# Output projection of a two-layer decoder trunk: the last quarter's weights split once into big tiles, and one more norm step on VectorE

## The chip, the cores and the metric

The kernel runs on one core of one Trainium2 chip. The metric is the device time of one execution in microseconds (us). Before the change the median of three runs is 2775.11 us (2769.86 to 2777.68).

## The reference

The program is a decoder trunk of two layers on a sequence of 1024 tokens with 1024 channels, float32. Each layer has a token mixer and a channel mixer. What matters here is the end of the first and the start of the second:

```python
mix = jnp.einsum('bsd,de->bse', merged, w_o)            # output projection, 1024 x 1024 x 1024
x = layer_norm(ALPHA * x + mix, ln1_g, ln1_b)           # over the 1024 channels of each token
up = causal_dwconv(jnp.einsum('bsd,df->bsf', x, w_up), ffn_conv_w)   # 1024 x 5632
```

`layer_norm` subtracts the mean, divides by the root of the variance plus 1e-5, multiplies by a gain and adds a bias. There are two layers, so everything told below happens twice.

## The kernel before, in words

**Products in three passes.** A float32 operand is split into a rounded high half and a low half (`split`, lines 87 to 94): ScalarE (ACT) copies the source into a tile of the rounded type (line 90), then VectorE (DVE) or GpSimd (POOL) subtracts that copy from the source (line 94). A product is then three matmuls: high by high, high by low, low by high (`product`, lines 106 to 112).

**Tiles.** Every kind of tile has a fixed number of buffers: 14 of kind X (two 128 x 1024 halves each), 6 of kind w (one 128 x 1024 half, or both halves of a 128 x 512 block), 3 of kind ws (a loaded weight, 128 x 1024). PSUM has 8 banks of 128 x 512. A new tile takes a buffer whose last reader is done; its first writer waits for that.

**Output projection** (`output`, lines 628 to 671). There are eight token tiles t of 128 tokens, in two halves h of four. For each h the merged operand is split into four X tiles (`mt`). For each half of the output columns, eh, four accumulators collect over four weight blocks kp; a weight block is loaded by SyncE's queue (SP) into a ws tile, ACT makes the high half and POOL the low half, into two w tiles (`weight`, lines 96 to 104, called at line 645). So three of the four quarters (h, eh) load four blocks each. In the last quarter, h = 1 and eh = 1, the four token tiles are taken in two pairs, (4, 5) and then (6, 7), and each pair loads and splits the four blocks again: eight loads, eight high halves, eight low halves.

After a quarter with eh = 1 the token tiles are normalised (`norm`, lines 262 to 292). DVE adds alpha times the residual (line 663), takes the statistics (259, 267), subtracts the mean and multiplies by the gain (290); ACT takes the root (269); DVE refines the reciprocal in four short steps (271, 274 to 277); ACT multiplies by it (291); and the bias is added (292), for t = 7 by DVE and for the other seven by POOL. Norms are marked urgent, so the planner ranks them far ahead of their place in the text.

**The hand-over to the up projection.** The up projection is Strassen-like: its moving operands are 512 x 512 blocks and sums of blocks of the normalised tokens, transposed by TensorE and split. Tokens 0 to 3 give two blocks (`to_first`, B11 and B21, four X tiles in all). Tokens 4 to 7 give five (`to_second`, lines 311 to 326: T1, T2, B22, T3, T4, ten X tiles): per token three subtractions on DVE (321, 323, 324) and one on POOL (322) into two w tiles, then five groups of four transposes (298), each into a PSUM bank of its own, from which ACT takes a high and DVE a low half. Only when all four tokens have gone through it can the second part of the first pair run, since its matmuls move all 512 tokens.

The order on TensorE (PE) and on SP is that of the text. After the last quarter it is: first part of weight pair 0 (`begin`, line 716: 24 matmuls, on B11 and B21, one low half by POOL and one by DVE, and one bank added up at line 730); `to_second` for token 4; first part of pair 1; `to_second` for tokens 5, 6 and 7; second part of pair 0 (`rest`, line 732: four sums of weight blocks on POOL at lines 741 and 738, five more blocks split by `made`). The first weight of each pair and the second one are loaded at line 707 into ws tiles. The orders of DVE, ACT and POOL are made by a planner from ranks in the text and its own estimate of times, and are then fixed.

Of the kernel before, what the change touches and what calls it, by code (L numbers as in the profile page):

```python
# [11 lines left out]
F32 = mybir.dt.float32  # L12
F32R = mybir.dt.float32r
# [5 lines left out]
P = 128  # L19
# [41 lines left out]
class Trunk:  # L61
# [566 lines left out]
    def output(self, l, merged):  # L628

        nc = self.nc  # L630
        self.xc = {}
        zs, st = [None] * 8, {}
        for h in range(2):
            mt = []
            for kp in range(NKP):
                t = self.new([P, 2, 2, HALF], F32R, "X")
                self.split(t[:, 0], t[:, 1], merged[kp][:, :, h * HALF:(h + 1) * HALF])
                mt.append(t)
            for eh in range(2):

                groups = [(0, 1), (2, 3)] if h and eh else [(0, 1, 2, 3)]
                for group in groups:
                    acc = {}
                    for kp in range(NKP):
                        wh, wl = self.weight(self.ins["w_o"][l, eh, kp])
                        if kp == NKP - 1 and eh == 0:
                            for t in range(4 * h, 4 * h + 4):
                                zs[t] = self.new([P, D], F32, ("pt", "pt", "pt", "q", "s", "s", "s", "t")[t])
                                nc.sync.dma_start(zs[t][:], self.ins["x"][t] if l == 0 else self.spill[t])
                            if h == 0:  # L650
                                g, b = self.gains(l, 0)
                        for t in group:
                            if t not in acc:
                                acc[t] = self.bank()
                            ts = slice(t * P, (t + 1) * P)
                            self.product(acc[t][:], [
                                (mt[kp][:, 0, k, ts], mt[kp][:, 1, k, ts], wh[:, k * HALF:(k + 1) * HALF],
                                 wl[:, k * HALF:(k + 1) * HALF]) for k in range(2)], kp == 0, kp == NKP - 1)
                        if (kp or eh) and group[0] == 0:
                            self.pending()  # L660
                    for t in group:
                        z = zs[4 * h + t][:, eh * HALF:(eh + 1) * HALF]
                        nc.vector.scalar_tensor_tensor(z, z, ALPHA, acc[t][:], op0=ALU.mult, op1=ALU.add)
                        st[4 * h + t] = self.stats(zs[4 * h + t], (eh,), st.get(4 * h + t))
                    if eh:
                        for i in group:
                            t = 4 * h + i
                            with self.urgent():
                                self.norm(zs[t], g, b, "vector" if t == 7 else "gpsimd", st[t])
                            self.pend.append((lambda t=t, i=i: self.to_second(zs[i], zs[t], i, self.spill1[t])) if h else  # L670
                                             (lambda t=t, i=i: self.to_first(zs[t], i, self.spill1[t])))

# [428 lines left out]
```

## Time and profile before

| | before |
|---|---|
| median of 3 runs | 2775.11 us |
| profiled execution, its own time | 2775.4 us |
| its span | 2773.4 us |
| PE busy, share of the span | 93% |
| DVE, ACT, POOL busy | 69%, 44%, 53% |
| granted clock of PE, mean | 0.971 of full |

Times in the trace count from the start of the span. "Idle before" is the time that an engine stood still ahead of an instruction, and the arrow names what ended it. A line number is that of the program; 90 and 94 belong to the splitting helper, so the tile names tell what is split. The output projection of the first layer ends near 677 us and that of the second near 2055 us.

### The profile page before, as it was taken

The numbers are of one execution on the slowest core, as the hardware profiler recorded it, in microseconds if no ns is written. First come the engines' busy times: TensorE is split into PE (matmuls) and PEld (weight loads), VectorE is DVE, ScalarE is ACT, GpSimd is POOL, SyncE is SP. The second block draws the span as 40 slices with busy tenths as digits, with TensorE's granted clock in tenths as the row PEclk, the third lists the DMA queues.
The fourth block names the chain that finished last, engine by engine and source line by source line (L and its number), as shares of the span: only waits on it lengthen the run. The fifth ranks groups of instructions, "written<-read, shape, count | busy, mean of one in ns | idle before, by whom it ended". The sixth has DMA issues, their size and how long they took to land.

```text
span 2773.4 us, 32010 instructions
## 1 busy us (share of the span) xinstructions
PE 2583.8 (93%) x11408; PEld 2105.9 (76%) x11408; DVE 1919.5 (69%) x2310; ACT 1233.4 (44%) x2050; POOL 1457.2 (53%) x962
## 2 busy tenths in 40 slices
PE   5989999998899999899889999999988999998887
PEld 4868887787688888677667788777867888877676
DVE  6565556737887877786675656477478887767866
ACT  4434445523544554434444444454335455544343
POOL 2554456767466555370434545566674556553701
PEclk8999999999999999999899999999999999999999
DMA  3433358554133333674323423765532333327742
GB/s 123 138 114 107 108 196 225 161 181 150 57 104 114 114 99 107 222 277 134 106 95 117 142 75 108 237 189 164 201 122 75 96 107 103 114 92 266 267 139 76
DMA packets 163232, 389.59 MB, mean 140 GB/s; under 512 B 17408, under 2 KB 48896, under 8 KB 162048
## 3 DMA queue, kind: packets, MB, share of 16 engines
q1 hardware_dynamic: 136496, 293.02, 32.3%
q0 software_dynamic: 14848, 55.09, 7.0%
q10 hardware_dynamic: 11728, 39.45, 3.7%
q8 instruction: 89, 1.46, 0.2%
q14 instruction: 71, 0.58, 0.1%
HBM read 281.75 MB, written 104.43 MB: 139 GB/s over the span
## 4 chain that ended last, share of the span: by engine, by line
PE 49%; DVE 16%; issue 5%; DMA 3%; ACT 3%; POOL 3%; ACTq 0%; DVEq 0%; SPq 0%; POOLq 0%
PE b L111 16%; PE b L112 16%; PE b L110 16%; DVE w L94 3%; DVE X L94 2%; DVE st L259 1%; DVE ve L275 1%; DMA X<-in_w_down 1%; POOL ws L738 1%; DVE pt L811 1%; ACT w L90 1%; POOL w L94 1%; DVE t L290 1%; DMA X<-h_blocks 1%; DVE w L321 0%
## 5 line engine op out<-in xcount | busy, mean ns | idle before, releaser
L110 PE MATMUL b<-X,w 128*128 128x512 f32 x2552 | 1014.1, 397 | 55.1 <-ACT s L727 20.0
L112 PE MATMUL b<-X,w 128*128 128x512 f32 x2552 | 1008.3, 395 | 27.9 <-DVE w L94 18.6
L111 PE MATMUL b<-X,w 128*128 128x512 f32 x2552 | 1006.5, 394 | 3.2 <-DVE X L94 3.2
L94 DVE TENSOR_TENSOR w<-ws,w 128x512 fp32r<-128x512 f32 (+1 forms) x454 | 450.4, 996 | 358.5 <-ACT w L90 346.3
L90 ACT CAST w<-ws 128x512 fp32r<-128x512 f32 (+1 forms) x608 | 408.0, 677 | 489.6 <-PE b L112 154.5
L110 PEld LDWEIGHTS b<-X,w 128*128 128x128 f32 x2552 | 487.4, 191 | 167.5 <-ACT s L727 24.6
L112 PEld LDWEIGHTS b<-X,w 128*128 128x128 f32 x2552 | 486.9, 191 | 136.4 <-DVE w L94 22.5
L94 POOL TENSOR_TENSOR w<-ws,w 128x512 fp32r<-128x512 f32 (+2 forms) x154 | 297.5, 1934 | 532.5 <-ACT w L90 520.3
L111 PEld LDWEIGHTS b<-X,w 128*128 128x128 f32 x2552 | 487.3, 191 | 105.9 <-DVE X L94 5.5
L741 POOL TENSOR_TENSOR ql<-ws 128x512 f32<-128x512 f32 x82 | 125.0, 1524 | 354.8 <-DMA ws<-in_w_in 254.0
L111 PE MATMUL b<-w,w 128*128 128x512 f32 x528 | 214.4, 406 | 48.5 <-DVE w L94 41.3
L110 PE MATMUL b<-w 128*128 128x512 f32 x528 | 211.1, 400 | 2.7 <-DVE pt L905 1.4
L112 PE MATMUL b<-w,w 128*128 128x512 f32 x528 | 210.6, 399 | 0.0
L111 PEld LDWEIGHTS b<-w,w 128*128 128x128 f32 x528 | 102.0, 193 | 82.4 <-DVE w L94 54.3
L738 POOL TENSOR_TENSOR ws<-ws,ws 128x512 f32<-128x512 f32 x82 | 142.4, 1736 | 6.2
L811 DVE SCALAR_TENSOR_TENSOR q<-t,par,q 128x1023 f32<-128x1023 f32 x88 | 127.4, 1448 | 19.0 <-ACT q L808 18.1
L94 DVE TENSOR_TENSOR w<-X,w 128x512 fp32r<-128x512 f32 (+1 forms) x107 | 121.5, 1158 | 22.3 <-ACT w L90 22.3
L738 POOL TENSOR_TENSOR ws<-ql,ws 128x512 f32<-128x512 f32 x82 | 125.0, 1524 | 6.3
L738 POOL TENSOR_TENSOR ws<-ws 128x512 f32<-128x512 f32 x82 | 118.6, 1446 | 16.9 <-DVE w L94 12.7
L110 PEld LDWEIGHTS b<-w 128*128 128x128 f32 x528 | 102.0, 193 | 28.3 <-DVE t L905 2.7
L811 DVE SCALAR_TENSOR_TENSOR pt<-t,par,pt 128x1023 f32<-128x1023 f32 x88 | 123.3, 1401 | 0.2
L112 PEld LDWEIGHTS b<-w,w 128*128 128x128 f32 x528 | 102.1, 193 | 20.6
(242 smaller groups left out, 3783.6 us busy)
## 6 DMA issues: line engine op xcount, KB each, us to landing
ws<-in_w_up SPq DMA_DIRECT2D x88, 512.0 KB
ws<-in_w_in SPq DMA_DIRECT2D x75, 512.0 KB
gates<-t ACTq DMA_DIRECT2D x48, 512.0 KB
ws<-in_w_o SPq DMA_DIRECT2D x40, 512.0 KB
h_blocks<-t SPq DMA_DIRECT2D x80, 256.0 KB
s<-h_blocks SPq DMA_DIRECT2D x66, 256.0 KB
t<-gates SPq DMA_DIRECT2D x32, 512.0 KB
t<-q_parts POOLq DMA_DIRECT2D x64, 256.0 KB, 4.1
```

What stands on the lines that cost most here:

```text
L90: self.nc.scalar.copy(hi, src)
L94: return eng.tensor_tensor(lo, src, hi.bitcast(F32), op=ALU.subtract)
L110: self.nc.tensor.matmul(out, wh, xh, start=start and i == 0, stop=False, skip_group_check=more)
L111: self.nc.tensor.matmul(out, wh, xl, start=False, stop=False, skip_group_check=more)
L112: self.nc.tensor.matmul(out, wl, xh, start=False, stop=stop and i == n - 1, skip_group_check=more)
L259: self.nc.vector.bn_stats(st[:, c, :], z[:, c * HALF:(c + 1) * HALF])
L275: nc.vector.scalar_tensor_tensor(ve[:], ve[:], r[:], r[:], op0=ALU.mult, op1=ALU.mult)
L290: nc.vector.scalar_tensor_tensor(z[:], z[:], mv[:, 0:1], g[:], op0=ALU.subtract, op1=ALU.mult)
L738: sub = lambda out, x, y: nc.gpsimd.tensor_tensor(out, x, y, op=ALU.subtract)
L741: nc.gpsimd.tensor_tensor(s1[:], a21, a22, op=ALU.add)
L811: nc.vector.scalar_tensor_tensor(y[:, d:], c[:, :S - d], w(k), y[:, d:], op0=ALU.mult, op1=ALU.add)
```

## The change

In the last quarter the four weight blocks are loaded by the first pair of token tiles into ws tiles as before, but their halves are made into one X tile per block, which is held, and the second pair uses the held halves. Nothing else of that quarter's order on PE changes. The number of loads in it falls from eight to four. And the bias of token tiles 4, 5 and 6 is added by DVE too, as it was for token tile 7.

```diff
-                groups = [(0, 1), (2, 3)] if h and eh else [(0, 1, 2, 3)]
+                groups, held = [(0, 1), (2, 3)] if h and eh else [(0, 1, 2, 3)], {}
                 for group in groups:
                     acc = {}
                     for kp in range(NKP):
-                        wh, wl = self.weight(self.ins["w_o"][l, eh, kp])
+                        if len(groups) == 1:
+                            wh, wl = self.weight(self.ins["w_o"][l, eh, kp])
+                        elif kp not in held:
+                            held[kp] = self.new([P, 2, 1024], F32R, "X")
+                            wt = self.new([P, 1024], F32, "ws")
+                            nc.sync.dma_start(wt[:], self.ins["w_o"][l, eh, kp])
+                            wh, wl = held[kp][:, 0], held[kp][:, 1]
+                            self.split(wh, wl, wt[:], "scalar", "gpsimd")
+                        else:
+                            wh, wl = held[kp][:, 0], held[kp][:, 1]
...
-                                self.norm(zs[t], g, b, "vector" if t == 7 else "gpsimd", st[t])
+                                self.norm(zs[t], g, b, "vector" if h else "gpsimd", st[t])
```

## Rows read from the trace of the kernel before

**Rows 1.** Windows, layer 0; columns PE, PEld, DVE, ACT, POOL, granted clock, DMA share.
```profile
622.00:644.00 22.00, 22.00 (x102) 18.26 (x102) 18.68 (x36) 9.39 (x13) 13.89 (x6) 1.00 0.51 199
...
682.00:704.00 22.00, 17.86 (x66) 14.07 (x67) 22.00 (x32) 5.99 (x11) 17.11 (x10) 0.73 0.09 38
704.00:724.00 20.00, 14.36 (x75) 10.59 (x75) 16.81 (x27) 11.03 (x22) 1.29 (x1) 0.84 0.20 71
724.00:755.00 31.00, 30.44 (x132) 24.61 (x130) 24.07 (x23) 16.42 (x25) 15.59 (x10) 0.99 0.13 40
```

**Rows 2.** Timeline of PE, layer 0: start, length, engine, line, tiles, idle before and releaser.
```profile
647.79 0.50 PE L111 MATMUL b<-w,X 128*128 128x512 f32 x1 [2.47 <-POOL w L94]
...
676.47 0.39 PE L112 MATMUL b<-w,X 128*128 128x512 f32 x1
...
682.36 0.79 PE L112 MATMUL b<-X,w 128*128 128x512 f32 x1 [4.61 <-POOL w L94]
682.96 0.63 PE L110 MATMUL b<-X,w 128*128 128x512 f32 x1
683.38 0.63 PE L111 MATMUL b<-X,w 128*128 128x512 f32 x1
...
691.11 1.04 PE L298 MATMUL b<-ident,w 128*128 128x128 f32 x8
...
698.93 0.80 PE L110 MATMUL b<-X,w 128*128 128x512 f32 x1 [3.72 <-DVE X L94]
...
719.10 0.80 PE L112 MATMUL b<-X,w 128*128 128x512 f32 x1 [3.09 <-DVE w L94]
```

**Rows 3.** The same of PE in layer 1.
```profile
2060.45 0.79 PE L112 MATMUL b<-X,w 128*128 128x512 f32 x1 [4.61 <-POOL w L94]
...
2097.18 0.79 PE L112 MATMUL b<-X,w 128*128 128x512 f32 x1 [3.73 <-DVE w L94]
```

**Rows 4.** Timeline of POOL, layer 0.
```profile
638.97 2.39 POOL L292 TENSOR_TENSOR pt<-pt,t 128x1024 f32<-128x1024 f32 x1 [1.28 <-ACT pt L291]
...
675.50 5.14 POOL L292 TENSOR_TENSOR s<-s,t 128x1024 f32<-128x1024 f32 x2 [2.80 <-ACT s L291]
680.60 1.71 POOL L94 TENSOR_TENSOR w<-ws,w 128x512 fp32r<-128x512 f32 x1
```

**Rows 5.** Timeline of ACT, layer 0.
```profile
642.86 1.03 ACT L90 CAST w<-ws 128x1024 fp32r<-128x1024 f32 x1
...
674.27 2.19 ACT L291 ACTIVATE s<-s,r 128x1024 f32<-128x1024 f32 x2 [4.66 <-DVE r L277]
676.36 1.12 ACT L90 CAST w<-ws 128x512 fp32r<-128x512 f32 x2
```

**Rows 6.** Timeline of SP's queue, layer 0: issues of the loads.
```profile
624.95 39.32 SPq L102 DMA_DIRECT2D ws<-in_w_o  x8
666.66 88.97 SPq L707 DMA_DIRECT2D ws<-in_w_up  x8
```

**Rows 7.** Timeline of DVE, layer 0.
```profile
639.08 2.30 DVE L275 SCALAR_TENSOR_TENSOR ve<-ve,r 128x1 f32<-128x1 f32 x1
...
672.77 0.14 DVE L276 TENSOR_SCALAR ve<-ve 128x1 f32<-128x1 f32 x1
672.83 1.27 DVE L290 SCALAR_TENSOR_TENSOR s<-s,mv,t 128x1024 f32<-128x1024 f32 x1
...
678.36 2.82 DVE L321 TENSOR_TENSOR w<-s,pt 128x512 f32<-128x512 f32 x1
...
694.92 3.30 DVE L290 SCALAR_TENSOR_TENSOR t<-t,mv,t 128x1024 f32<-128x1024 f32 x1
...
702.41 1.21 DVE L292 TENSOR_TENSOR t<-t,t 128x1024 f32<-128x1024 f32 x1
...
706.27 0.68 DVE L321 TENSOR_TENSOR w<-t,q 128x512 f32<-128x512 f32 x1
...
707.59 6.06 DVE L94 TENSOR_TENSOR X<-b,X 128x512 fp32r<-128x512 f32 x10
```

## The prediction, made before the changed kernel ran

> **What bounds the kernel now.** PE is busy for 93% of the span, so the first question is where it is not. I read the windows of layer 0 around the end of the output projection first. From 622 to 644 us and again from 724 on PE is full (22.00 of 22, 30.44 of 31) at a granted clock of 1.00 and 0.99; from 682 to 724 it is busy 32.2 of 42, at 0.73 and 0.84 [rows 1]. That hand-over to the up projection is the only place that the change can speed up much. In it DVE is busy 22.00 of 22 and then 16.81 of 20, POOL 17.11 and then 1.29 [rows 1].
>
> PE's timeline says what it waits for [rows 2]. The last matmul of the output projection starts at 676.47, so PE is through at about 676.7. It waits 4.61 until 682.36 for POOL's low half of pair 0's first weight; 3.72 until 698.93 for DVE (a low half out of PSUM, by which a bank comes free); 3.09 until 719.10 for DVE (the low half of a weight of the second part of pair 0). Behind each wait matmuls start 0.42 apart instead of 0.23 (682.96 and 683.38, against 132 instructions in 30.44 us [rows 1, 2]): the lower of the two clock levels, 1.2 GHz; at 682.36 some 13 matmuls do, 13 x 0.2 = 2.6 us. Layer 1 is the same: its first wait ends at 2060.45, its last at 2097.18 [rows 3], 36.7 apart as in layer 0. So the stretch to shorten is 676.7 to 719.1, 42.4 us, twice.
>
> Why is POOL late at 677? Its low half of pair 0 starts at 680.60, behind the bias additions of tokens 4 and 5 (two in 5.14 us from 675.50) [rows 4]. These waited for ACT's multiplication at 674.27, and ACT for DVE's reciprocal; ACT's high halves for pair 0 stand behind it, at 676.36 [rows 5]. The load itself was issued at 666.66, after the eight of the last quarter, which had been spread over 39.32 us from 624.95 on [rows 6]. Inside the last quarter PE waits for no weight after 647.79 [rows 2]: the four repeated splits are not on its path. What they cost is what stands behind them and beside them.
>
> Beside them means DVE. The subtraction of line 321 took 2.82 us at 678.36 while POOL added biases, and 0.68 at 706.27 with POOL idle; line 290 took 3.30 at 694.92 and 1.27 at 672.83 [rows 4, 7].
>
> **The change, part by part.** The numbers are us per layer.
>
> *Four repeated loads, four high halves, four low halves less.* ACT loses 4 x 1.03 = 4.1 (a cast [rows 5]), POOL 4 x 2.39 = 9.6 (taken at the addition of the same size [rows 4]), SP four loads of 512 KB. On PE's path directly: nothing.
>
> *The load of pair 0 comes earlier.* It is moved past four loads. The four that go stood in the later part of the 39.32 us [rows 6]; as an estimate from that, it is issued some 14 us earlier, about 653 instead of 666.66, and 24 us ahead of PE's need. The held halves use no w tiles, so pair 0's four halves find w buffers when PE leaves the third quarter (about 653) instead of near 677. So the 4.61 wait goes, with its 2.6 of low clock: PE ends pair 0's first part at 676.7 + 24 x 0.23 = 682.2, where it started it at 682.36.
>
> *Held X tiles.* Live then are four of `mt`, four of B11 and B21 and four held: 12 of 14 buffers. `to_second` takes ten more, which must wait for PE's last output matmul; its transposes are behind that on PE anyway. Cost nothing; cover: PE's own order.
>
> *Three bias additions from POOL to DVE.* DVE gets 3 x 1.21 = 3.6 [rows 7], POOL loses three of 2.57, 7.7 (two in 5.14 [rows 4]). The trace has this form on DVE uncontended only; beside POOL an operation of this size took 3.30 at the most [rows 7], so the bounds are 3.6 and 9.9; I take 3.6, since POOL has then little to do. Each addition waits on DVE for ACT's multiplication (1.1, two in 2.19 [rows 5]); queued behind it are the other subtractions and, behind those, PE's banks. If the planner leaves nothing to fill in, that is 3 x 1.1 = 3.3; I take 0 to 3.3, nearer 0, as two tokens are always in work.
>
> *DVE's debt when PE is done, 676.7.* Now PE no longer waits for POOL, so DVE is what is late next. With POOL out of the way, tokens 4 and 5 can be normalised before 676.7: in 664 to 677.6 DVE has to put two additions (2.4), the three subtractions of token 4 (2.0) and two low halves (1.4), 5.8, into room made by shorter operations and idle time there. What is left: 20 low halves of transposes at 0.60 (ten in 6.06), 12.0; the norms of tokens 6 and 7, each 2 x 0.65 (accumulator, statistics, of the size of line 321) + 1.27 + 1.21 + six short steps of 0.14, 4.6, so 9.2; three times three subtractions at 0.65, 5.9; two additions of banks and the first low half of the second part, 1.9 [rows 7]. Sum 29.0. The same list for before (no addition for 6, one more token's subtractions, three more weight halves) is 31.7, and it took from 677.6 to 719.1, 41.5: 9.8 more, beside about 22 us of POOL work (17.11 [rows 1] and 5 before 682), or 0.45 us for each us of POOL. After the change POOL has three subtractions (line 322) and perhaps one low half there, 4 x 1.7 = 6.8 [rows 4], so 3.0. The second part of pair 0 then starts at 676.7 + 29.0 + 3.0 = 708.7 instead of 719.1: a gain of 10.4. What follows is PE at 30.44 of 31 [rows 1], so it is kept.
>
> The Trainium skill, SBUF — State Buffer, section "SBUF: two separate sides", says that VectorE with two SBUF inputs and GpSimd share a pair of ports as an exclusive lock held for a whole instruction, and that the other fully blocks. By that, each of the four POOL instructions could hold DVE for its full 1.7, 6.8 instead of 3.0, and the gain would be 6.6 a layer, 2762; the 2.82 of line 321 beside the additions agrees with it.
>
> **Sum.** Two layers of 10.4 are 20.8. The profiled execution took 2775.4 (span 2773.4), 0.3 above the median of 2775.11; 2775.1 - 20.8 = 2754.3, say 2755.
>
> Bounds: PE alone needs from 676.7 on 48 x 0.23 + 80 transposes at 0.13 (eight in 1.04 [rows 2]) = 21.4, and behind the last of them 3.6 of low halves on DVE: 701.7, a gain of 17.4 a layer, 2740. The other end is below.
>
> **The rivals.** *Absorbed.* PE arrives early and waits at DVE instead: the 3.72 and 3.09 waits, both DVE's, grow by what the 4.61 gives up. For it: DVE was full from 682 to 704 and had no pause until about 721 [rows 1]. It needs that DVE's work isn't thinned: the planner lays POOL's sums for pair 0 (four of 1.7) under the norms, and the additions cost their waits (3.6 + 3.3 against 9.8 of stretch). Gain 0 to 4 a layer: 2767 to 2775. Against it: most of the stretch stood beside POOL's additions and low halves, and these leave.
>
> *The stall moves up, slower.* Place: 628 to 648, the norms of tokens 0 to 3, whose bias additions stay on POOL. The first two loads of the last quarter are issued from 624.95 on [rows 6]. Before, their halves had to wait for w tiles; now X tiles are free as soon as the first half is done (about 623), so the planner can put two low halves of 2.39 on POOL amid these norms, where DVE is already busy 18.68 of 22 [rows 1]. There a one-element step on DVE took 2.30 at 639.08, beside POOL's addition at 638.97 of 2.39 [rows 4, 7]. The cast of the weight that PE waits 2.47 for at 647.79 stands behind the last of these norms, at 642.86 [rows 2, 5]. Price: 2 x 2.39 = 4.8 more wait and 2.6 of low clock behind it, 7.4 a layer. It decides where the hand-over gives less than 7.4: with what the absorbed case gives (0 to 4), 2782 to 2790; with the forecast's 10.4 it leaves 2769. Against it: the half that PE needs first ranks first, and POOL has pauses of 1.3 between these additions [rows 4]. The rule of the lock cited above would make this place worse, not better.
>
> *It does not do what it says.* A held tile finds no X buffer, or the planner makes the halves as late as before: then loads and splits are saved off the path alone, 2775. The count of 12 in 14 speaks against it.
>
> **How the numbers follow.** Forecast 0.62 (its own range 2740 to 2765); absorbed 0.20; stall moves up 0.14; not as told 0.04. A measurement of this kernel tells about 0.3% from no change, 8.3 us. Faster by more than that: the forecast's 0.62 and 0.06 of the absorbed case, 0.68. Within: 0.14 of the absorbed, 0.04, and 0.01 of the moved stall, 0.19. Slower: 0.13. The range goes from a little below PE's floor to the lower part of the moved stall, 2738 to 2782.
>
> **What would show it.** Right: no wait for POOL at the first matmuls of pair 0; its load near 653; line 321 of token 4 before 677 and near 0.7; the second part of pair 0 some 32 us behind the end of the output projection, not 42. Wrong: waits for DVE before it that add up to the old 42; a wait near 648 above 2.47; additions on DVE with idle time before them that ends with ACT's line 291. The prediction fails if DVE's work from 677 on still takes about 40 us with POOL idle, which would say that its order and not POOL held it.

## The result and the profile after

| | before | after |
|---|---|---|
| median | 2776.39 us (6 runs, 2769.86 to 2779.35) | 2756.07 us (6 runs, 2752.76 to 2759.53) |
| ratio after / before | | 0.9931, 95% interval 0.9917 to 0.9944 |
| profiled execution, its own time | 2775.4 us | 2757.35 us |
| its span, mean granted clock | 2773.4 us, 0.971 | 2755.5 us, 0.976 |

The ratio is 19.2 us of 2776, with an interval of 15.5 to 23.0: faster. The forecast was 2755.

PE's timeline of the changed kernel shows where it came from: layer 0, then the last two rows from layer 1 (start, length, engine, line, tiles, idle before and its releaser; line numbers behind 640 are 9 higher than before).

```profile
648.71 0.79 PE L111 MATMUL b<-w,X 128*128 128x512 f32 x1 [2.45 <-POOL w L94]
649.30 0.63 PE L112 MATMUL b<-w,X 128*128 128x512 f32 x1
...
678.92 0.39 PE L112 MATMUL b<-X,X 128*128 128x512 f32 x1
...
684.60 1.04 PE L298 MATMUL b<-ident,w 128*128 128x128 f32 x8
...
692.19 0.50 PE L110 MATMUL b<-X,w 128*128 128x512 f32 x1 [2.48 <-DVE X L94]
...
705.84 0.63 PE L298 MATMUL b<-ident,w 128*128 128x128 f32 x4 [2.01 <-DVE w L323]
...
711.34 0.50 PE L112 MATMUL b<-X,w 128*128 128x512 f32 x1 [1.74 <-DVE w L94]
...
2046.91 0.39 PE L112 MATMUL b<-X,X 128*128 128x512 f32 x1
...
2079.16 0.80 PE L112 MATMUL b<-X,w 128*128 128x512 f32 x1 [2.48 <-DVE w L94]
```

The wait of 4.61 for POOL [rows 2] is gone: the output projection's last matmul starts at 678.9, pair 0's first part follows at once, and token 4's transposes start at 684.60. The wait for a bank is 2.48 instead of 3.72, the last one 1.74 instead of 3.09. Between them the kernel before waited 1.66 for another bank and 0.57 for a DVE subtraction of token 7; now these are 0.52 and 2.01.

I take as the length of the hand-over the time from the start of the output projection's last matmul to the start of the third matmul of pair 0's second part, the one behind the last wait (in the kernels where that wait is gone, the same matmul): 676.5 to 719.1 before, 42.6 us in layer 0 and 42.6 in layer 1 (2054.6 to 2097.2); after the change 678.9 to 711.3, 32.4, and 2046.9 to 2079.2, 32.2. Together 20.6 us, the whole gain: the stretch between the two hand-overs takes 1335.5 us before and 1335.6 after, and what follows the second one 676.2 and 676.3. About two thirds of it are shorter waits of PE (14.1 to 6.8 in layer 0, 14.4 to 7.6 in layer 1); the rest is PE's own work, at a granted clock of 0.83 and 0.84 before and 0.89 and 0.94 after. This length is a better measure than the span of one execution: the executions profiled below reach the last matmul of the output projection of layer 0 anywhere between 674.1 and 685.5 us.

The wait at 648.71 is as before (2.45, 2.47 [rows 2]), but here PE ran at the low clock behind it (0.63 long, starts 0.42 apart), in layer 1 not; before it was the other way round. From the end of this wait to the output projection's last matmul it takes 30.2 us here and 28.7 before. With 0.9 us of differences ahead of the wait, that puts the last matmul of layer 0 at 678.9 instead of 676.5.

SP's queue and POOL, the same kernel:

```profile
625.88 25.46 SPq L650 DMA_DIRECT2D ws<-in_w_o  x4
653.36 94.38 SPq L716 DMA_DIRECT2D ws<-in_w_up  x8
```
```profile
648.60 7.22 POOL L94 TENSOR_TENSOR X<-ws,X 128x1024 fp32r<-128x1024 f32 x3
656.11 2.39 POOL L94 TENSOR_TENSOR X<-ws,X 128x1024 fp32r<-128x1024 f32 x1 [0.28 <-ACT X L90]
658.46 1.29 POOL L94 TENSOR_TENSOR w<-ws,w 128x512 fp32r<-128x512 f32 x1
663.20 1.29 POOL L750 TENSOR_TENSOR ql<-ws 128x512 f32<-128x512 f32 x1 [3.46 <-DMA ws<-in_w_up]
...
675.64 2.15 POOL L322 TENSOR_TENSOR w<-s 128x512 f32<-128x512 f32 x1 [7.04 <-DVE s L292]
677.74 1.75 POOL L94 TENSOR_TENSOR w<-ws,w 128x512 fp32r<-128x512 f32 x1
...
696.88 1.28 POOL L322 TENSOR_TENSOR w<-t 128x512 f32<-128x512 f32 x1 [4.21 <-DVE X L94]
```

The first load of the up projection goes at 653.36 instead of 666.66 [rows 6]; POOL has pair 0's half ready at 659.75 instead of 682.3 [rows 4], and the four sums for its second part (from 663.20 on, 1.3 each) lie ahead of the norms of tokens 4 and 5, where DVE waits for PE. Before, they lay between 682 and 691, beside DVE's norms and subtractions.

DVE, the same kernel:

```profile
671.64 1.28 DVE L290 SCALAR_TENSOR_TENSOR s<-s,mv,t 128x1024 f32<-128x1024 f32 x1
...
674.27 2.36 DVE L292 TENSOR_TENSOR s<-s,t 128x1024 f32<-128x1024 f32 x2 [1.09 <-ACT s L291]
676.55 1.79 DVE L321 TENSOR_TENSOR w<-s,pt 128x512 f32<-128x512 f32 x1
678.37 1.67 DVE L323 TENSOR_TENSOR w<-s,w 128x512 f32<-128x512 f32 x1
...
686.54 1.27 DVE L290 SCALAR_TENSOR_TENSOR t<-t,mv,t 128x1024 f32<-128x1024 f32 x1
```

Line 290 takes 1.28 and 1.27 where it took up to 3.30 [rows 7]; the two additions moved to DVE take 2.36 together. Token 4's lines 321 and 323 are stretched (1.79 and 1.67), beside POOL's line 322 at 675.64 and the low half at 677.74. The windows of the hand-over (PE, PEld, DVE, ACT, POOL, granted clock):

```profile
679.00:701.00 22.00, 18.87 (x98) 15.15 (x96) 21.41 (x39) 9.03 (x17) 5.42 (x4) 0.92 0.12 49
701.00:712.00 11.00, 7.17 (x40) 5.35 (x39) 10.72 (x19) 7.61 (x15) 0.00 (x0) 0.84 0.00 0
```

DVE is still busy almost throughout (32.1 of 33), but POOL beside it 5.4 us instead of 17.11 in 22 [rows 1]. Over the whole hand-over of layer 0, DVE's busy time falls from 41.5 to 31.5 us and POOL's from 23.9 to 5.5.

### The profile page after: what moved, and what is told of

It is laid out like the page before. It is cut to its first block, busy times and chain, and to the rows that moved or that the text cites. A ratio compares the mean times of both kernels' runs of the same rounds, so it can differ in the third digit from the quotient of the medians.

```text
span 2755.5 us, 31972 instructions
## 1 busy us (share of the span) xinstructions
PE 2572.8 (93%) x11408; PEld 2099.2 (76%) x11408; DVE 1903.3 (69%) x2316; ACT 1224.8 (44%) x2042; POOL 1418.5 (51%) x948
## 3 DMA queue, kind: packets, MB, share of 16 engines
q1 hardware_dynamic: 135344, 288.82, 32.2%
## 4 chain that ended last, share of the span: by engine, by line
PE 57%; DVE 18%; DMA 8%; issue 7%; ACT 5%; POOL 4%; ACTq 0%; SPq 0%; DVEq 0%; POOLq 0%
PE b L111 19%; PE b L112 19%; PE b L110 19%; DVE w L94 4%; DMA X<-in_w_down 2%; DVE X L94 2%; ACT s L509 1%; DMA X<-h_blocks 1%; POOL ws L747 1%; DVE st L259 1%; DVE pt L820 1%; ACT X L90 1%; DVE m L500 1%; ACT w L90 1%; DMA ws<-in_w_down 1%
## 5 line engine op out<-in xcount | busy, mean ns | idle before, releaser
L90 ACT CAST w<-ws 128x512 fp32r<-128x512 f32 (+1 forms) x592 | 391.4, 667 | 453.9 <-PE b L112 149.2
L94 POOL TENSOR_TENSOR w<-ws,w 128x512 fp32r<-128x512 f32 (+1 forms) x138 | 257.1, 1864 | 521.5 <-ACT w L90 509.6
L112 PEld LDWEIGHTS b<-w,w 128*128 128x128 f32 x528 | 102.4, 194 | 20.8
```

Source lines behind the costliest of these rows:

```text
L90: self.nc.scalar.copy(hi, src)
L94: return eng.tensor_tensor(lo, src, hi.bitcast(F32), op=ALU.subtract)
L112: self.nc.tensor.matmul(out, wl, xh, start=False, stop=stop and i == n - 1, skip_group_check=more)
```

## The experiments

Ratios are to the kernel before, in the same rounds; lengths are of the hand-over as defined above, layer 0 / layer 1, from each kernel's profile.

| kernel | median us | ratio, 95% interval | hand-over us |
|---|---|---|---|
| before | 2776 to 2777 | 1 | 42.6 / 42.6 |
| adds_only | 2773.04 | 0.9983, 0.9973 to 0.9993 | 40.2 / 40.2 |
| held_only | 2764.48 | 0.9955, 0.9942 to 0.9968 | 37.3 / 37.3 |
| late_load | 2764.88 | 0.9959, 0.9947 to 0.9971 | 36.8 / 35.5 |
| again_low | 2769.81 | 0.9971, 0.9958 to 0.9983 | 36.5 / 35.0 |
| kp3_first | 2754.69 | 0.9919, 0.9906 to 0.9932 | 35.3 / 35.5 |
| twice_322 | 2768.38 | 0.9968, 0.9955 to 0.9981 | 35.1 / 34.6 |
| all_adds | 2750.25 | 0.9903, 0.9890 to 0.9916 | 33.5 / 33.8 |
| **the change** | 2756.07 | 0.9931, 0.9917 to 0.9944 | 32.4 / 32.2 |
| vec_322 | 2755.68 | 0.9923, 0.9911 to 0.9934 | 31.5 / 31.5 |
| adds_vec322 | 2751.06 | 0.9911, 0.9895 to 0.9927 | 31.2 / 31.8 |
| adds_w2pool | 2751.65 | 0.9908, 0.9895 to 0.9920 | 30.8 / 30.8 |
| adds_w2pool_u0 | 2767.06 | 0.9962, 0.9947 to 0.9976 | 29.4 / 29.6 |
| all_four | 2766.76 | 0.9964, 0.9951 to 0.9978 | 29.2 / 28.6 |

### Each half of the change alone

**held_only**, against the changed kernel:

```diff
-self.norm(zs[t], g, b, "vector" if h else "gpsimd", st[t])
+self.norm(zs[t], g, b, "vector" if t == 7 else "gpsimd", st[t])
```

> Only the weights of the last quarter are held; the bias of tokens 4 to 6 stays on POOL. Theory (the load and the halves of pair 0 come early, and DVE is thinned because POOL's repeated halves leave): moving the additions is worth about nothing, since the 3.6 us that DVE gains are the 0.45 x 7.7 us of stretch that POOL's additions put on it, so nearly the whole gain is here, 8 to 10 us a layer, 2756 to 2760 us, and the load of pair 0 is issued at about 653 us as in the changed kernel. Rival (POOL's additions, in front of pair 0's half and beside DVE's subtractions, are what made the 42 us): 0 to 4 us a layer, 2768 to 2776 us.

**adds_only**, against the kernel before, is the same line the other way:

```diff
-self.norm(zs[t], g, b, "vector" if t == 7 else "gpsimd", st[t])
+self.norm(zs[t], g, b, "vector" if h else "gpsimd", st[t])
```

> Only the bias of tokens 4 to 6 moves to DVE; the last quarter loads and splits its four blocks twice as before. Theory: pair 0's load still goes at about 667 us and its high halves at about 676, the wait for POOL shrinks from 4.61 to 1 to 2 us, and DVE pays as much as it saves: 1 to 3 us a layer, 2769 to 2774 us. Rival (the additions on POOL were the cause): 6 to 10 us a layer, 2756 to 2764 us.

Held weights alone are worth 12.5 us by the ratio, 5.3 us of hand-over a layer, between my theory and the rival. The additions alone are worth 4.7 us (2.4 a layer), inside the 1 to 3 a layer that I expected; the wait for POOL at pair 0 shrinks to 1.23, as expected, but another one of 2.90 for POOL follows it. Together the hand-over falls by 10.3, more than 5.3 + 2.4, in both layers: each needs the other. (By the ratios, 12.5 + 4.7 against 19.2 with an interval of 15.5 to 23.0, this would not be clear of noise; and the profile of held_only is of the longest of its six executions, 2772.99 us.) PE and then DVE of held_only show why:

```profile
699.78 0.76 PE L110 MATMUL b<-X,w 128*128 128x512 f32 x1 [7.44 <-DVE X L94]
```
```profile
679.38 0.69 DVE L321 TENSOR_TENSOR w<-s,pt 128x512 f32<-128x512 f32 x1 [3.57 <-POOL s L292]
...
681.81 2.77 DVE L324 TENSOR_TENSOR w<-w,pt 128x512 f32<-128x512 f32 x1
684.50 1.77 DVE L94 TENSOR_TENSOR w<-ws,w 128x512 fp32r<-128x512 f32 x1
...
693.51 2.72 DVE L324 TENSOR_TENSOR w<-w,pt 128x512 f32<-128x512 f32 x1
```

The 4.61 wait for POOL is gone there too and the load goes at 656.03, but PE now waits 7.44 for a bank instead of 3.72. DVE stood 3.57 for POOL's addition of token 4 (2.40 on POOL, against about 1.2 on DVE), and then ran beside the next one (2.83 on POOL), 2.77 for a subtraction of 0.68. This is the prediction's absorbed case in part, and the moved additions are what lifts it.

### What in holding the weights pays: the load or POOL's time

**late_load**: in the second pair, each block is loaded again and ACT writes its high half over the held one, so the loads and ACT's work of before are back, but not POOL's.

```diff
 else:
+    wt = self.new([P, 1024], F32, "ws")
+    nc.sync.dma_start(wt[:], self.ins["w_o"][l, eh, kp])
     wh, wl = held[kp][:, 0], held[kp][:, 1]
+    nc.scalar.copy(wh, wt[:])
```

> The changed kernel, but the second pair of tokens loads each block again and ACT writes the same high half into the held tile again, which must wait for the first pair's matmuls; POOL's low halves are made once. So the load of pair 0 goes at 664 to 667 us again instead of 653, with POOL still free of the repeated halves and the w tiles free. Theory (the early load is not needed as such; pair 0's half only has to be ready at 679, and POOL free): the first wait does not come back, pair 0's four sums on POOL come to lie beside the norms of tokens 4 and 5 and cost 1 to 3 us a layer, 2757 to 2762 us. Rival (the lateness of the load is what holding the weights cures): most of the 6 us a layer that the held weights alone gave is lost, 2765 to 2769 us.

**again_low**: the other half, POOL's work without the loads.

```diff
 else:
     wh, wl = held[kp][:, 0], held[kp][:, 1]
+    zero = self.mask_r[:, 0, P:P + 1].bitcast(F32).to_broadcast([P, 1024])
+    nc.gpsimd.tensor_tensor(wl, wl.bitcast(F32), zero, op=ALU.subtract)
```

> The changed kernel, but POOL goes over each held low half once more for the second pair (it subtracts a zero in place, so the values stay), which must wait for the first pair's matmuls: POOL's repeated work of the kernel before is back, without its loads, without ACT's casts and without w tiles. The load of pair 0 stays early, near 653 us. Theory (holding pays through both the early load and POOL's free time, in that POOL's sums for pair 0 come before the norms): about 8 us of POOL push the sums beside the norms of tokens 4 and 5, 1 to 4 us a layer, 2758 to 2764 us, hand-over 33 to 36 us. Rival A (POOL's repeated halves are the whole cost of the old way): 2766 to 2769 us, hand-over 37 or more. Rival B (only the load's place counts): 2755 to 2757 us, hand-over 32.

late_load costs 4.4 and 3.3 us of hand-over, 2764.88 us in all: above the theory's 1 to 3, a shade below the rival's band. The first wait did not come back (pair 0's half on POOL is at 671.74, in time); the loss is on DVE. Its rows, then POOL's:

```profile
677.27 2.20 DVE L292 TENSOR_TENSOR s<-s,t 128x1024 f32<-128x1024 f32 x1
679.40 1.25 DVE L275 SCALAR_TENSOR_TENSOR ve<-ve,r 128x1 f32<-128x1 f32 x1
...
682.87 1.24 DVE L277 TENSOR_TENSOR r<-r,ve 128x1 f32<-128x1 f32 x1
...
685.33 1.62 DVE L292 TENSOR_TENSOR s<-s,t 128x1024 f32<-128x1024 f32 x1 [0.62 <-ACT s L291]
```
```profile
676.63 1.76 POOL L753 TENSOR_TENSOR ql<-ws 128x512 f32<-128x512 f32 x1 [3.60 <-DMA ws<-in_w_up]
678.47 2.16 POOL L750 TENSOR_TENSOR ws<-ws,ws 128x512 f32<-128x512 f32 x1
680.71 1.69 POOL L750 TENSOR_TENSOR ws<-ql,ws 128x512 f32<-128x512 f32 x1
```

POOL's sums for pair 0 stand at 676 to 684, each with a stretched DVE step beside it (one-element steps of 1.25 and 1.24). The order on DVE changed as well (token 5's last statistics start at 674.94 instead of 669.19), so the 4 us are not the sums' alone; I have not separated the two.

again_low costs 4.1 and 2.8 us of hand-over. PE's new stalls for POOL in the last quarter are small beside it (0.55 in layer 0, 1.71 in layer 1). DVE, beside three of POOL's passes in a row (6.58 us from 669.02):

```profile
669.09 2.90 DVE L290 SCALAR_TENSOR_TENSOR s<-s,mv,t 128x1024 f32<-128x1024 f32 x1
...
672.04 3.57 DVE L275 SCALAR_TENSOR_TENSOR ve<-ve,r 128x1 f32<-128x1 f32 x2
```

In the changed kernel these are 1.23 and 0.34. Its sums for pair 0 were still early (662 to 669), not pushed beside the norms as the theory had it: here it is the repeated work itself that stands beside the norms. The median is 2769.81: of the 11 us that it loses by the ratios, hand-overs and stalls make 9.2, the rest is within the intervals. The hand-over is near the theory's (36.5 and 35.0 against 33 to 36), the time at rival A's (2766 to 2769).

Both parts of holding pay, then, the early load and POOL's free time. What the two runs lose adds up to 8.5 us of hand-over in layer 0 and 6.0 in layer 1, about what adds_only, which has neither part, loses against the change (7.8 and 8.0). In both runs the loss stands on DVE beside POOL's work on SBUF; in late_load that is not shown to be all of it.

### The price of POOL beside DVE

**twice_322** issues POOL's subtraction of `to_second` twice, **vec_322** puts it on DVE:

```diff
-nc.gpsimd.tensor_tensor(t3, y[:, HALF:], y[:, :HALF], op=ALU.subtract)
+for _ in range(2):
+    nc.gpsimd.tensor_tensor(t3, y[:, HALF:], y[:, :HALF], op=ALU.subtract)
```
```diff
-nc.gpsimd.tensor_tensor(t3, y[:, HALF:], y[:, :HALF], op=ALU.subtract)
+nc.vector.tensor_tensor(t3, y[:, HALF:], y[:, :HALF], op=ALU.subtract)
```

> The changed kernel, with POOL's subtraction of line 322 issued twice for each of tokens 4 to 7: four more POOL instructions of 1.3 to 1.8 us a layer beside DVE's work in the hand-over, and nothing else. Theory by the prediction's term (0.45 us of DVE for each us of POOL beside it): 3 us a layer, 2762 us. Rival A (each stands in DVE's way for its whole length): 5 to 7 us a layer, 2766 to 2770 us. Rival B (POOL does not stretch the path at all): 2756 us.

> The changed kernel, with line 322's subtraction on DVE instead of POOL. DVE gets 4 x 0.65 = 2.6 us a layer more, POOL leaves the stretch almost wholly. Theory (0.45): 3.0 saved against 2.6, 2755 us. Rival A (whole length): 6 saved against 2.6, 3 to 4 us a layer won, 2748 to 2750 us. Rival B (no stretch): 2.6 us a layer lost, 2761 us.

twice_322 adds four instructions of 1.3 to 1.9 us on POOL in each hand-over, 6.7 us, and the hand-over grows by 2.7 and 2.4: 0.40 and 0.36 us for each us of POOL, near the 0.45 of the prediction and far from the whole length. The time, 2768.38, looked like rival A all the same, and the reason is a mistake in both expectations: `to_second` also prepares layer 1's input projection, so there are three such places and not two. From the first load of the down projection of layer 0 to the start of the last matmul of layer 1's output projection, twice_322 takes 936.8 us against 933.2, 3.6 more, and at the transposes there PE waits 3.60 for DVE at 1412.68 where the changed kernel has a wait of 0.57. 2.7 + 2.4 + 3.6 = 8.7 of the 10.3 us by the ratios. vec_322 gives 0.9 and 0.7 in the two hand-overs, more than 0.4 x 6.8 against 2.6 of DVE work would (0.1); in time it is the same as the change. By the windows POOL's time in layer 0's hand-over falls there from 5.5 to 0.6, and three of the four subtractions lie in it on DVE, 1.8 together: an estimate from that is (0.9 + 1.8) / 4.9, 0.55 us for each us of POOL that leaves. So the price was between 0.36 and 0.55 here, and not one constant. Rival A's 3 to 4 a layer is not in the hand-overs.

DVE and POOL of twice_322 show how the average comes about:

```profile
679.48 1.66 DVE L324 TENSOR_TENSOR w<-s,w 128x512 f32<-128x512 f32 x1
681.17 1.67 DVE L325 TENSOR_TENSOR w<-w,pt 128x512 f32<-128x512 f32 x1
682.76 0.68 DVE L673 SCALAR_TENSOR_TENSOR s<-s,b 128x512 f32<-128x512 f32 x1
...
686.12 2.19 DVE L290 SCALAR_TENSOR_TENSOR s<-s,mv,t 128x1024 f32<-128x1024 f32 x1
...
701.89 7.20 DVE L94 TENSOR_TENSOR X<-b,X 128x512 fp32r<-128x512 f32 x11 [0.33 <-ACT X L90]
```
```profile
680.55 1.74 POOL L94 TENSOR_TENSOR w<-ws,w 128x512 fp32r<-128x512 f32 x1
685.95 3.50 POOL L323 TENSOR_TENSOR w<-s 128x512 f32<-128x512 f32 x2 [3.66 <-PE b L112]
...
700.82 2.64 POOL L323 TENSOR_TENSOR w<-t 128x512 f32<-128x512 f32 x2 [3.41 <-PE b L112]
```

Operations with two operands in SBUF wait (1.66, 1.67 for 0.68; 2.19 for 1.27). The low halves out of PSUM do not: the first three of the eleven at 701.89, beside POOL's last pair, take 1.89 together, the same as three low halves of weights at 715.60 with POOL idle.

The Trainium skill, SBUF — State Buffer, section "SBUF: two separate sides", states the lock for VectorE instructions with two SBUF inputs. In the rows shown here the traces agree, instruction by instruction. A sum made from whole lengths, as the prediction's sentence on it had (2762), came out too large here, for two reasons that the rows show. Part of DVE's work reads PSUM. And POOL waits too: its line 322 takes 1.28 at 696.88 in the changed kernel, beside a low half out of PSUM, and 2.15 at 675.64, where DVE's additions run until 676.6, so the 1.7 taken as its length holds some of its own waiting.

### Trying to gain more

**all_adds** puts the bias of tokens 0 to 3 on DVE too, **kp3_first** ranks the split that PE waits for at 648 ahead of the norms:

```diff
-self.norm(zs[t], g, b, "vector" if h else "gpsimd", st[t])
+self.norm(zs[t], g, b, "vector", st[t])
```
```diff
-wh, wl = self.weight(self.ins["w_o"][l, eh, kp])
+with self.tc.high_priority(offset=2000 if h and kp == NKP - 1 else 0):
+    wh, wl = self.weight(self.ins["w_o"][l, eh, kp])
```

> The changed kernel, and the bias of tokens 0 to 3 is added by DVE too. Theory (POOL's additions stretch DVE's short steps there, 2.3 us at 639 us in the trace of before): four times 1.21 us more for DVE against some 6 us of stretch that goes, so the wait at 648 us falls from 2.45 to 0.5 to 2 us and 0 to 3 us a layer are won, 2749 to 2757 us. Rival (DVE's own work is what makes the norms late): the wait grows to 4 to 7 us with low clock behind it, 2760 to 2770 us.

> The changed kernel, and the split of the last weight block of the third quarter ranks ahead of the norms of tokens 0 to 3. Theory (that block's high half waits on ACT only for its place behind the norms, from about 629 us when its w tiles come free to 644): the wait of 2.45 us at 648 and the 1 to 2 us of low clock behind it go, 3 to 4 us a layer, 2747 to 2751 us. Rival (the half would wait for something else, or takes the norms' place and makes the first tokens late): no gain, 2755 to 2760 us, with a wait at the transposes of the first tokens instead.

Both remove the wait of 2.45 at 648 in both layers. kp3_first, at 2754.69 near its rival's 2755 to 2760 and not at the theory's 2747 to 2751, keeps almost nothing of it: PE comes 2.5 us earlier to a DVE that does not, the wait for the bank grows from 2.48 to 4.62, the hand-over from 32.4 to 35.3. all_adds gives back 1.1 to 1.6 of the hand-over and keeps the rest: 2750.25, inside the 2749 to 2757 of its theory, although the wait fell to nothing and not to 0.5 to 2. Its ratio lies below that of the change, the intervals just fail to touch (0.9916 and 0.9917). The two waits of 2.45 and 1.5 of low clock behind one of them, less 2.7 of hand-over, are 3.7 us of the 5.8 between the medians; where the rest lies is not traced.

**adds_w2pool** is all_adds with the low half that PE waits for last made by POOL in pair 0 (`early` is set for pair 0 of the up projection alone), **adds_vec322** all_adds with vec_322's edit, **adds_w2pool_u0** ranks ACT's copy of a pair's first product ahead in addition to adds_w2pool, **all_four** has everything:

```diff
-w2 = self.made(a11)
+w2 = self.made(a11, "gpsimd" if early else "vector")
...
-nc.scalar.copy(u[:, 0, :], a[:])
+with self.urgent():
+    nc.scalar.copy(u[:, 0, :], a[:])
```

> The changed kernel, with the bias of tokens 0 to 3 on DVE too (2750 us when run alone) and the first low half of the second part of the up projection's pair 0 made by POOL, which stands idle there from about 694 us, instead of DVE. Theory (PE's last wait of 2.50 us is for that half, which stands behind all low halves of the transposes on DVE): the wait goes with its low clock, 2 to 4 us a layer, 2743 to 2747 us. Rival (the next thing on DVE, the last transposes' halves, ends as late, or the chain only moves): 2749 to 2751 us.

> The changed kernel with the bias of tokens 0 to 3 and line 322's subtraction on DVE too. If the two gains add (some 3 us a layer by the first, 1 us for each of three hand-overs by the second): 2744 to 2749 us. Rival (DVE is now what each hand-over waits for throughout, and the second adds its 2.6 us of work): 2750 to 2756 us.

> The kernel with the bias of tokens 0 to 3 on DVE and pair 0's first low half on POOL, and ACT's copy of a pair's first product ranked ahead of the up projection's scaling. Theory (the second edit's 2.8 us were given back two pairs later, where PE waited 3.71 us for that copy and ran at the low clock behind it): that wait goes, 2740 to 2747 us. Rival (the wait comes back at the next thing that ACT does late, or the new rank disturbs other pairs): 2749 to 2758 us.

> All of it together: bias of all eight tokens on DVE, line 322 on DVE, pair 0's first low half on POOL, and ACT's copy of a pair's first product ranked ahead. If the gains add: 2737 to 2745 us. Rival (they are bounded by the same DVE work): 2746 to 2752 us.

adds_w2pool removes its wait (the hand-over is 2.7 to 3.0 shorter than that of all_adds) and the time stays (0.9908 against 0.9903), as its rival had it. PE's rows say where it went:

```profile
742.49 0.80 PE L110 MATMUL b<-X,w 128*128 128x512 f32 x1 [3.71 <-ACT s L736]
743.08 0.63 PE L111 MATMUL b<-X,w 128*128 128x512 f32 x1
743.51 0.63 PE L112 MATMUL b<-X,w 128*128 128x512 f32 x1
```

all_adds waits 1.30 at this place (pair 2) and goes on at the high clock; here the wait is 3.71, and matmuls behind it start 0.43 apart. 2.4 longer wait and the low clock give the gain back. Ranking that copy ahead did not cure it: in adds_w2pool_u0 the wait is still 3.7, and the kernel is slower by 15 us, outside both of its expectations; of the 11.4 us between the two profiled executions, some 10 are there before the output projection of layer 0 ends (685.3 against 675.3). The rank acts on all pairs, the input projection's too; what it disturbs there I did not follow up. all_four has the same rank and the same time, 2766.76, also outside both of its expectations, so it does not tell whether the gains add. adds_vec322 does: its hand-overs are 2.3 and 2.0 shorter than those of all_adds, but its time is no better (0.9911 against 0.9903). In its profiled execution the stretches between and behind the hand-overs are 4.1 and 3.7 longer; why, I did not follow. The lowest median here is that of all_adds; adds_vec322 and adds_w2pool cannot be told from it.

## Why the prediction was right

*PE no longer waits for POOL at pair 0.* Right: the load at 653.36 against the 653 given, no wait there, its cost taken as 4.61 and the low clock.

*DVE is then what is late.* Right: every wait left in the hand-over names DVE, and DVE is busy 32.1 of 33 us. The length: 708.7 - 676.5 = 32.2 predicted, 32.4 and 32.2 measured; two layers 20.8 predicted, 20.6 by the traces and 19.2 (15.5 to 23.0) by the ratio. Shown is the mechanism: with POOL's time in layer 0's hand-over down from 23.9 to 5.5 us, DVE is busy 31.5 us instead of 41.5, of which the sum's lists put only 2.7 (31.7 to 29.0) to less work. DVE's order alone did not hold it at 42. The exactness is partly luck, since errors cancelled. The sum had all of token 4's subtractions and two low halves done before PE was; in the run two of these subtractions, at 676.55 and 678.37, ran beside POOL (together 2.1 longer than at their clean length), and the third and one of the low halves came behind PE's end, at 680.07 and 681.27. Against that, less of POOL's work than the 6.8 us taken lies behind that point (5.4 from 679 on). So the sign that line 321 of token 4 would take near 0.7 failed: it took 1.79.

*0.45 us of DVE for each us of POOL.* A figure read from one stretch; twice_322 has 0.40 and 0.36, vec_322 some 0.55. Right within its use, as an average.

*Three bias additions from POOL to DVE.* The term's own price was right (2.36 for two, 3.6 for three). A sign that was given for wrong did show, small: DVE stood 1.09 for ACT's line 291 ahead of the additions at 674.27, before PE was done, within the 0 to 3.3 given. But what the move is worth was never worked out alone. My later expectation, that on top of the held weights it is worth nothing, was wrong by 5 us a layer (37.3 against 32.4 and 32.2): the addition on POOL is also a link in the chain of token 4, and DVE, in order, stood behind it for 3.57.

*Held tiles cost nothing.* No wait in the trace contradicts it; PE has none in the last quarter.

*The rivals.* The moved stall did not come: the wait at 648 is 2.45, and POOL's held halves start at 648.60, behind the norms as before. The absorbed case came in part in held_only, not in the change. The third, that the load or the halves come no earlier, is refuted by the load at 653.36.

## What to carry to other kernels

When the same operand is prepared twice, ask what stands behind and beside the second preparation, and not only whether the consumer waits for it: here PE waited for none of the repeated halves, and the gain was that the next stage's load went 13 us earlier and that POOL left DVE's instructions with two operands in SBUF alone. Where an in-order engine is full until a hand-over ends, count its remaining work from the moment the producer is done; here that sum gave the time, with errors in it that cancelled, and edits that only brought PE there earlier came back as longer waits. Two halves of a change can need each other: test each alone before dropping one.

## What the runs showed of the hardware

The same wait is followed by either clock level: 2.45 us at 648.71 with starts 0.42 apart behind it, the lower level, and 2.47 in the kernel before [rows 2] with starts 0.23 apart; in layer 1 the reverse. From the end of this wait to the output projection's last matmul it is 30.2 or 28.7 us, so the price of the low clock behind a wait of this length was 0 or some 1.5 us here, not a constant.

POOL and DVE stretched each other where DVE's instruction had two operands in SBUF: in late_load a one-element DVE step took 1.25 us at 679.40, beside a POOL subtraction, and 0.21 at 674.81 with POOL idle; in the changed kernel POOL's 128x512 subtraction took 2.15 beside DVE's additions and 1.28 beside a low half out of PSUM. DVE's low halves out of PSUM kept their length beside POOL in twice_322.
